# Gate and up projections of a two-layer diffusion block: eight-product pairs first, weight sums earlier, seven activations split ahead

## The chip, the cores and the metric

One core of one Trainium2 chip runs the whole program. The metric is the device time of one execution in microseconds (us).

## The reference, cut to what matters

The reference is a two-layer transformer block for 512 latent and 256 context tokens with a model width of 1024. Each layer normalises and modulates the tokens, mixes them with two attention branches, and adds a gated SwiGLU feed-forward with 2816 inner channels:

```python
def swiglu(h, w_gate, w_up, w_down):
    return (jax.nn.silu(h @ w_gate) * (h @ w_up)) @ w_down
...
h2 = modulate(rms_norm(x, norm2_g[l]), sh2, sc2)
x = x + gt2 * swiglu(h2, w_ffn_gate[l], w_ffn_up[l], w_ffn_down[l])
```

Layer 0 does this for 768 tokens, layer 1 (the last) for the 512 latent ones. The change lies in `h @ w_gate`, `h @ w_up` and in the passage to `@ w_down`.

## The kernel before, in words

Each layer runs `mixers` (projections and attention), `merge`, `project` (the output projection, one half of the tokens after the other), `gate_up` and `down`. Every matrix product is made of three matmuls on operands split into a high and a low part: ScalarE (ACT) copies the high part, VectorE (DVE) subtracts it from the value to get the low part. The order of the work on each engine is written out by hand, and each engine and each queue works through its own list in order.

The 22 tiles of 128 inner channels are called pairs here: gate tile f and up tile f. Two token halves (384 columns each in layer 0, 256 in layer 1) times gate and up make a 2x2 block, and `gate_up` computes it by a scheme of seven products in place of eight. A product is 12 matmuls (`prod`, line 1282; four tiles of the inner dimension, three matmuls each). The scheme needs sums and differences of weights, `prep_s` (DVE, lines 1330 and 1331) and `prep_s2` (GpSimd, POOL, lines 1336 and 1337, in place on the raw gate weights, so it has to wait until `prep_g` has read them), and sums and differences of the two token halves, the operands T1 to T4 (lines 1450 to 1455, 1516). Their splits are `prep_g`, `prep_13`, `prep_24` and `prep_a22` for weights, `high` and `low` (lines 1227 to 1232) for tokens. The evacuations are `ev_...`; S[f] holds a pair's tiles.

When `project` ends, the first token half is already normalised (`norm_half`: operands 11 and 21), the second is not. So lines 1459 to 1539 begin with the products of four pairs (`EARLY`) that need 11 and 21 alone, and prepare meanwhile everything else: `times` normalises the second half, `diff` forms the differences, then T2, T3, 22, T1, T4 follow. The loop over f (line 1558) comes after that; up to f = 3 it has an order of its own (`early`, `mixed`), from f = 4 one iteration issues on TensorE (PE) q6, r7, q5 of pair f, p1 of pair f+1, p3 of f, p2 of f+1, r4 of f. In it `prep_s(nf)` stands behind `prep_a22(f)`, `prep_s2(nf)` behind q5, and `prep_24(nf)`, which splits the result for the next q6, behind p1.

A finished pair is stored to DRAM (`store`, on the SyncE queue, SP). In the last pairs the first five (`AHEAD`) are read back and split (`act`); `down` reads pairs 5 and 6 back, then eight residual tiles `x`, then the first tiles of the next group, and runs three groups of pairs times eight output tiles (`down_group`). Raw weights lie in three slots "wf" that the weight queue `W`, the raw gate tiles and, in layer 0, the `ada` tiles share: `background` reads one `ada` tile (modulation weights of later stages, 56 of them in `ada_tiles`) and makes its dot products on DVE for the tile before. Layer 0's `down_group` runs all that are left ahead of the last group (line 1198).

Of the kernel before, what the change touches and what calls it, by code (L numbers as in the profile page):

```python
# [19 lines left out]
P = 128  # L20
# [14 lines left out]
EARLY = 4  # L35
AHEAD = 5
# [85 lines left out]
class Kernel:  # L122
# [60 lines left out]
    def weight_order(self, l):  # L183
        a, W = self.a, self.W
        idx = {m: i for i, m in enumerate([0, 1, 2, 3, 4, 6, 7, 8, 9, 10] + list(range(12, 28)))}
        win = lambda m: W.add(a["w_in"][l, idx[m]])
        for m in (4, 0, 1, 2):
            win(m)
        for m in range(2):
            W.add(a["w_v"][l, m])  # L190
        for m in (3, *range(12, 20), 10, 6, 7, 8, 9, *range(20, 28)):
            win(m)
        for m in range(8):
            W.add(a["w_proj"][l, m])
        for _ in range(2):
            for m in range(8):
                W.add(a["w_out"][l, m])
        if FAST[l]:
            for f in range(EARLY):
                W.add(a["w_gu"][l, 2 * f])  # L200
        for g, (f0, fn) in enumerate(GROUPS):
            for f in range(2 * f0, 2 * (f0 + fn)):
                if not FAST[l]:
                    W.add(a["w_gu"][l, f])
            for _ in range(2 if g == len(GROUPS) - 1 else 1):
                for m in range(8):
                    W.add(a[f"w_dn{g}"][l, m])
# [1038 lines left out]
    def norm_half(self, l, n, c0, c1):  # L1246
# [3 lines left out]
        self.H = {op: [None] * 4 for op in ("11", "21", "22", "T1", "T2", "T3", "T4")}  # L1250
# [22 lines left out]
    def gate_up(self, l, last, n, tq):  # L1273
# [81 lines left out]
        def q6(f):  # L1355
            early = f < EARLY
            if early:
                S[f]["a"] = self.wide("a")[:, :hw]
            prod(S[f]["a"], S[f]["S24"], 0, "T2", early)
# [31 lines left out]
        def ev_sum(f, cs):  # L1391
            if cs is lo_:
                S[f]["t"] = self.unit("t")
            t = S[f]["t"][:, cs]
            if f < EARLY:
                nc.vector.tensor_tensor(t, S[f]["a"], S[f]["s"][:, hi_], ALU.add)
            else:
                nc.scalar.activation(t, S[f]["a"], AF.Copy)
# [9 lines left out]
        def ev_c12(f):  # L1408
            s = S[f]["s"][:, hi_]
            if f < EARLY:  # L1410
                nc.vector.tensor_tensor(s, S[f]["a"], s, ALU.add)
                s = S[f]["s"][:, :n]
                nc.scalar.activation(s, s, AF.Silu)
            else:
                nc.scalar.activation(s, S[f]["a"], AF.Silu)
# [11 lines left out]
        ws = {}  # L1427

        def first(f, k):
            if k == 0:  # L1430
                ws[f] = self.W.get(1 if f < 2 else -1)
                S[f]["e"] = self.bank("e")[:, :hw]
            prod(S[f]["e"], ws[f], 512 * k, "21" if k else "11", k == 0)

        def first_evac(f, k):
            if k == 0:
                S[f]["s"] = self.unit("s")
            nc.scalar.activation(S[f]["s"][:, lo_ if k else hi_], S[f]["e"], AF.Copy)

        t, tt = [None] * KD, []  # L1440

        def times(i, eng=nc.scalar):
            t[i] = (self.tq.tile([P, hw], F32, name=self.nm("t"), tag="t", bufs=15) if i < KD - 1 else self.unit("t"))[:, :hw]
            nc.vector.tensor_tensor(t[i], xt[i][:, c0:c1], rb[:, :hw], ALU.mult)
            self.modulated(l, i, t[i], c0, c1, eng)
            nc.sync.dma_start(out=self.xs[i][:, :n], in_=xt[i][:, :n])
            xt[i] = None

        def diff(j):
# [7 lines left out]

        J = range(4)
        first(0, 0)
        load_g(0)  # L1460
        load_u(0)
        load_u(1)
        first_evac(0, 0)
        self.flush()
        r = self.stats(c0, c1)
        first(1, 0)
        first_evac(1, 0)
        rb = self.spread(r, c0, c1)
        prep_s(0)
        prep_s2(0)  # L1470
        first(0, 1)
        first(1, 1)
        for i in (0, 4, 1, 5):
            times(i)
        first_evac(0, 1)
        self.W.split(self.W.at + 1)
        times(2)
        times(6, nc.gpsimd)
        diff(0)
        times(3)  # L1480
        times(7, nc.gpsimd)
        load_g(1)
        first_evac(1, 1)
        self.low("T2", 0, t0[0], hw)
        diff(1)
        first(2, 0)
        first_evac(2, 0)
        diff(2)
        new_24(0)
        split_high(S[0]["G"], S[0]["S24"])  # L1490
        self.low("T2", 1, t0[1], hw)
        first(3, 0)
        diff(3)
        self.low("T2", 2, t0[2], hw)
        first_evac(3, 0)
        self.low("T2", 3, t0[3], hw)
        split_low(S[0]["G"], S[0]["S24"])
        load_g(2)
        first(2, 1)
        first(3, 1)  # L1500
        new_13(0)
        split_high(S[0]["S"], S[0]["S13"])
        for j in J:
            self.high("T3", j, t[j], hw)
            self.low("T3", j, t[j], hw)
        first_evac(2, 1)
        split_low(S[0]["S"], S[0]["S13"])
        q6(0)
        r7(0)
        first_evac(3, 1)  # L1510
        for j in J:
            self.high("22", j, t[j + 4], hw)
            self.low("22", j, t[j + 4], hw, nc.gpsimd)
        ev_sum(0, lo_)
        for j in J:
            nc.gpsimd.tensor_tensor(t0[j + 4], t0[j + 4], t0[j], ALU.add)
            self.high("T1", j, tt[j], hw)
            self.low("T1", j, tt[j], hw)
        nc.scalar.activation(S[0]["t"][:, hi_], S[0]["d"], AF.Copy)
        prep_a22(0)  # L1520
        prep_s(1)
        prep_s2(1)
        q5(0)
        s, t_ = S[0]["s"][:, hi_], S[0]["t"][:, hi_]
        nc.vector.tensor_tensor(t_, t_, S[0]["a"], ALU.subtract)
        nc.vector.tensor_tensor(t_, t_, s, ALU.subtract)
        p3(0)
# [3 lines left out]
        prep_24(1)  # L1531
        tq.close()
        ev_c12(0)
        r4(0)
        prep_13(1)
        q6(1)
        ev_diff(0, lo_)
        ev_act(0)
        ev_sum(1, lo_)
        prep_s(2)  # L1540
        prep_s2(2)
        prep_24(2)
        r7(1)
        load_g(3)

        with self.tc.tile_pool(name="pa", bufs=1, side="right", reuse_waits="tile") as pa:
            raw = {}

            def prefetch(i):
                raw[i] = pa.tile([P, TOK], F32, name=self.nm("ar"), tag="ar", bufs=AHEAD)  # L1550
# [7 lines left out]
            for f in range(1, NF):  # L1558
                early, mixed = f < EARLY - 1, f < EARLY
                end = f == NF - 1  # L1560
                nf = f + 1
                if not mixed:

                    q6(f)
                    if end:
                        act(0)
                    silu1(f)
                    ev_diff(f - 1, lo_)
                    prep_g(nf)
                    r7(f)  # L1570
                    ev_sum(f, lo_)
                    ev_act(f - 1)
                    prep_a22(f)
                    prep_s(nf)
                    if end:
                        act(1)
                    q5(f)
                    prep_s2(nf)
                else:
                    q5(f)  # L1580
                    if f > 1:
                        ev_diff(f - 1, lo_)
                        ev_act(f - 1)
                    prep_a22(f)
                self.background(0 if last else 1)
                if early:
                    q6(nf)
                elif nf < NF:
# [3 lines left out]
                if end:  # L1592
                    self.W.prepare()
# [3 lines left out]
                if end:  # L1597
                    act(2)
                p3(f)
                if early:  # L1600
                    ev_sum(nf, lo_)
                    if f + 2 == EARLY:
                        prep_g(f + 2)
                    prep_s(f + 2)
                    r7(nf)
                elif nf < NF:
                    ev_s1(nf)
                    if not mixed:
                        prep_24(nf)
                    p2(nf)  # L1610
                ev_c12(f)
                if early:
                    prep_s2(f + 2)
# [3 lines left out]
                self.background(0 if last else f % 2 or f >= 12)  # L1617
                r4(f)
                if early:
                    prep_24(f + 2)  # L1620
                elif nf < NF:
                    ev_c11(nf)
                load_g(f + 3)
                store(f - 1)
                if f >= NF - AHEAD - 2 and f < NF - 2:
                    prefetch(f - (NF - AHEAD - 2))
            act(4)
            ev_diff(NF - 1, lo_)
            ev_act(NF - 1)
            store(NF - 1)  # L1630
# [3 lines left out]
    def down(self, l, last, n, chunks, halves, streams):  # L1634
# [16 lines left out]
        for f in range(AHEAD, first):  # L1651
            load(f)
        self.xt = []
        for m in range(8):
            x = self.unit("x")
            nc.sync.dma_start(out=x[:, :n], in_=self.xs[m][:, :n])  # L1656
            self.xt.append(x)
        for f in range(first, first + 2):
            load(f)
        for f in range(AHEAD, first):  # L1660
            ready(f)
        self.rate = int(not last)
        for g, (f0, fn) in enumerate(GROUPS):
            act, self.act = self.act[:fn], []

            def step(m):
                f = f0 + fn + m
                if g + 1 < len(GROUPS) and m < GROUPS[g + 1][1]:
                    load(f + 2)
                    ready(f)  # L1670
            self.down_group(l, last, chunks, halves, streams, g == len(GROUPS) - 1, act, step)
        if last:
# [104 lines left out]
```

## Time and profile before

| what | value |
|---|---|
| runs | 1983.65, 1981.83, 1981.61 us, median 1981.83 |
| the profiled execution | 1985.74 us, its span 1984.0 us |
| busy | PE 1854.6 us (93%), DVE 1411.3 (71%), ACT 978.0 (49%), POOL 696.1 (35%) |
| granted TensorE clock, mean | 0.972 of full speed |
| `gate_up`, layer 0 and layer 1 | from 597.8 to 958.5 us and from 1559.7 to 1839.1 us of the span |
| HBM traffic | 228.02 MB read, 34.34 MB written |

Times inside the program are us from the start of the span. PE is the engine with the most work, so what counts is where it stands idle or runs at the lower of its two clock levels (1.2 and 2.4 GHz); the 93% is a mean over stages in which it never waits and stages in which it waits often.

### The profile page before, as it was taken

The page shows a single profiled execution, that of the slowest core. Times are in us where ns is not written, and L with a number is a line of the kernel's source. Part 1 is how long each engine was busy: PE and PEld are TensorE (multiplying, and loading weights), DVE is VectorE, ACT ScalarE, POOL GpSimd, SP SyncE. Part 2 cuts the span into 40 slices and gives each one's busy share as a digit, 9 for nine tenths or more (in the row PEclk, how much of TensorE's full clock was granted, in tenths as well). Part 3 has the DMA queues.
Part 4 walks back from the last instruction along what each step waited for, and adds up shares of the span by engine and source line. Part 5 has one row for each costly group of instructions (what it writes and reads, how often), then busy time and mean ns, then how long its engine had stood idle before and what let it go on. Part 6 is the DMA issues. An engine that isn't in the chain of part 4 may idle for free. (4 is left out here: it accounts for less than half of the span.)

```text
span 1984.0 us, 31045 instructions
## 1 busy us (share of the span) xinstructions
PE 1854.6 (93%) x11680; PEld 1754.3 (88%) x11680; DVE 1411.3 (71%) x2403; ACT 978.0 (49%) x1851; POOL 696.1 (35%) x662
## 2 busy tenths in 40 slices
PE   7999999999997899999899999999999869989898
PEld 3889899989997799999799998888889869888688
DVE  6668878995567789998666576758866766666445
ACT  5458736775345243334322345857864534444333
POOL 3446536552245123222000353536523522332003
PEclk7999999999998899999899999999999979999999
DMA  7222232225433344556665532122145533333544
GB/s 277 94 98 83 89 114 82 68 70 207 139 124 141 122 150 151 153 176 203 242 205 171 164 129 77 59 68 70 43 148 186 173 101 107 119 132 124 201 133 138
DMA packets 86612, 264.37 MB, mean 133 GB/s; under 512 B 9744, under 2 KB 11824, under 8 KB 86336
## 3 DMA queue, kind: packets, MB, share of 16 engines
q1 hardware_dynamic: 79280, 248.68, 38.1%
q10 hardware_dynamic: 6992, 13.64, 1.8%
q8 instruction: 92, 1.51, 0.3%
q0 software_dynamic: 192, 0.08, 0.1%
q14 instruction: 56, 0.46, 0.1%
HBM read 228.02 MB, written 34.34 MB: 132 GB/s over the span
## 5 line engine op out<-in xcount | busy, mean ns | idle before, releaser
L73 ACT ACTIVATE wh<-wf 128x1024 fp32r<-128x1024 f32 (+1 forms) x175 | 181.6, 1039 | 254.5 <-PE d L575 147.7
L74 DVE TENSOR_TENSOR wl<-wf,wh 128x1024 fp32r<-128x1024 f32 (+1 forms) x141 | 174.0, 1235 | 93.3 <-ACT wh L73 91.1
L573 PE MATMUL d<-hh,wl 128*128 128x384 f32 (+2 forms) x640 | 235.7, 368 | 0.6 <-DVE q L849 0.4
L574 PE MATMUL d<-hl,wh 128*128 128x384 f32 (+2 forms) x640 | 224.5, 351 | 1.0 <-DVE hl L543 0.9
L575 PE MATMUL d<-hh,wh 128*128 128x384 f32 (+2 forms) x640 | 223.9, 350 | 0.0
L573 PE MATMUL d<-ah,wl 128*128 128x384 f32 (+2 forms) x592 | 201.2, 340 | 14.7 <-ACT ah L179 10.3
L1336 POOL TENSOR_TENSOR rawG<-rawG,S 128x512 f32<-128x512 f32 x44 | 71.7, 1629 | 394.6 <-DVE S L1331 195.1
L574 PE MATMUL d<-al,wh 128*128 128x384 f32 (+2 forms) x592 | 200.5, 339 | 1.7 <-DVE al L180 1.7
L575 PE MATMUL d<-ah,wh 128*128 128x384 f32 (+2 forms) x592 | 199.7, 337 | 0.0
L484 POOL TENSOR_TENSOR ssq<-ssq,sq 128x384 f32<-128x384 f32 (+1 forms) x48 | 68.3, 1423 | 355.3 <-ACT sq L480 339.5
L812 POOL TENSOR_SCALAR p<-p,rec 128x768 f32<-128x768 f32 (+3 forms) x160 | 131.5, 835 | 94.5 <-DVE rec L809 65.5
L459 DVE SCALAR_TENSOR_TENSOR junk<-wa,crow 128x1024 bf16<-128x1024 f32 x128 | 159.1, 1243 | 3.3 <-DMA wa<-w_ada 3.3
L1124 DVE SCALAR_TENSOR_TENSOR x<-d,mod,x 128x384 f32<-128x384 f32 (+3 forms) x144 | 70.5, 509 | 123.2 <-PE d L575 123.2
L1289 PE MATMUL a<-H,wh 128*128 128x384 f32 (+1 forms) x640 | 143.6, 314 | 0.0
L868 DVE TENSOR_TENSOR pt<-pt,pt 128x512 fp32r<-128x512 f32 (+1 forms) x192 | 123.9, 661 | 25.2 <-ACT pt L864 24.0
L573 PEld LDWEIGHTS d<-ah,wl 128*128 128x128 f32 x592 | 113.4, 192 | 21.0 <-ACT ah L179 11.1
L575 PEld LDWEIGHTS d<-hh,wh 128*128 128x128 f32 x640 | 121.0, 189 | 7.4
L574 PEld LDWEIGHTS d<-hl,wh 128*128 128x128 f32 x640 | 121.8, 190 | 5.3 <-DVE hl L543 2.2
L573 PEld LDWEIGHTS d<-hh,wl 128*128 128x128 f32 x640 | 121.7, 190 | 5.2 <-issue 0.9
L864 ACT ACTIVATE pt<-pt 128x512 fp32r<-128x512 f32 (+1 forms) x192 | 107.2, 577 | 31.5 <-PE pt L827 27.4
L749 POOL TENSOR_TENSOR qs<-q,qs 64x128 fp32r<-64x128 f32 x160 | 81.1, 507 | 116.0 <-ACT qs L748 54.6
L574 PEld LDWEIGHTS d<-al,wh 128*128 128x128 f32 x592 | 113.6, 192 | 8.0 <-DVE al L180 3.5
(239 smaller groups left out, 5447.6 us busy)
## 6 DMA issues: line engine op xcount, KB each, us to landing
wa<-w_ada SPq DMA_DIRECT2D x96, 512.0 KB, 3.6
wf<-w_in SPq DMA_DIRECT2D x52, 512.0 KB, 3.5
rawG<-w_gu SPq DMA_DIRECT2D x44, 512.0 KB, 4.7
rawU<-w_gu SPq DMA_DIRECT2D x44, 512.0 KB, 3.8
wf<-w_out SPq DMA_DIRECT2D x32, 512.0 KB, 3.5
wf<-w_dn SPq DMA_DIRECT2D x32, 512.0 KB, 3.5
wf<-w_dn SPq DMA_DIRECT2D x32, 448.0 KB, 4.5
act_scratch<-s SPq DMA_DIRECT2D x22, 384.0 KB, 4.9
```

Of the source, the lines that this page charges most:

```text
L73: high = lambda: self.nc.scalar.activation(hi[:, :n], t[:, :n], AF.Copy)
L74: low = lambda: (engine or (self.nc.vector if self.aux is None else self.nc.gpsimd)).tensor_tensor(lo[:, :n], t[:, :n], hi[:, :n], ALU.sub ...
L459: nc.vector.scalar_tensor_tensor(junk, t, 1.0, self.crow[:, s, :], ALU.mult, ALU.mult, accum_out=acc)
L573: nc.tensor.matmul(ps, wl[:, ks], xh[:, c0:c1], start=first, stop=False)
L574: nc.tensor.matmul(ps, wh[:, ks], xl[:, c0:c1], start=False, stop=False)
L575: nc.tensor.matmul(ps, wh[:, ks], xh[:, c0:c1], start=False, stop=last)
L749: nc.gpsimd.tensor_tensor(st[l0:l0 + 64, c], q[h0:h0 + 64], st[h0:h0 + 64, c], ALU.subtract)
L812: nc.gpsimd.tensor_scalar(pt, pt, rec[:, i:i + 1], 1.0, ALU.mult, ALU.mult)
L864: nc.scalar.activation(r[1][0], r[0], AF.Copy)
L868: nc.vector.tensor_tensor(r[1][1], r[0], r[1][0], ALU.subtract)
L1289: nc.tensor.matmul(ps, a[:, ks], b, start=first and j == 0 and i == 0, stop=j == 3 and i == 2, skip_group_check=True)
L1336: nc.gpsimd.tensor_tensor(G[:, :512], G[:, :512], s[:, :512], ALU.subtract)
```

## The change

In both layers pairs 0 and 1 (`PLAIN`) are computed with the usual eight products (`plain`: one weight tile, one token half, eight inner tiles, 24 matmuls), pairs 2 to 21 with seven. The two token halves need only their own normalised values for that, as operands 11, 21, 12 and 22; T1 to T4 and the weight sums come after. The special order for the first pairs goes away. In the loop `prep_s(nf)` moves to just behind q6(f) and `prep_s2(nf)` behind `prep_g(nf)`. In the last pair seven activations are split in place of five, through five raw slots; `down` then reads only two `x` tiles at first, one more at each step, and stores the last pair after those first loads. The `ada` tiles start at pair 4, run on through all three groups of `down` in layer 0, and are no longer run out ahead of the last group.

```diff
-EARLY = 4
-AHEAD = 5
+PLAIN = 2
+AHEAD = 7
+SLOTS = 5
...
-            for f in range(EARLY):
-                W.add(a["w_gu"][l, 2 * f])
+            for f in range(2 * PLAIN):
+                W.add(a["w_gu"][l, f])
...
         if end and not last:
-            self.background(len(self.bg) + 1)
-            self.rate = 0
+            while len(self.bg) > 32:
+                self.background(1)
...
+        def plain(i, half, ws, ps=None):
+            ps = self.bank("d")[:, :hw]
+            for k in range(KD):
+                x = H[("11", "12", "21", "22")[half + k // 4 * 2]][k % 4]
...
+                nc.tensor.matmul(ps, wl[:, ks], x[:, lo_], start=k == 0, stop=False)
+                nc.tensor.matmul(ps, wh[:, ks], x[:, hi_], start=False, stop=False)
+                nc.tensor.matmul(ps, wh[:, ks], x[:, lo_], start=False, stop=k == KD - 1)
...
+        w = [self.W.get(2 - i) for i in range(3)]
+        g = plain(0, 0, w[0])
+        for _ in range(4):
+            next(g)
+        load_g(PLAIN)
+        load_u(PLAIN)
+        load_u(PLAIN + 1)
+        self.flush()
+        r = self.stats(c0, c1)
+        drain(g)
+        evs.popleft()()
+        rb = self.spread(r, c0, c1)
+        g = plain(1, 0, w[1])
+        for k in range(KD + 2):
+            if k < KD:
+                times(k, (nc.gpsimd, nc.scalar)[k % 2])
+            if 1 <= k <= KD:
+                self.high("12" if k <= 4 else "22", (k - 1) % 4, t[k - 1], hw)
+            if k >= 2:
+                self.low("12" if k < 6 else "22", (k - 2) % 4, t[k - 2], hw)
+            if k == 2:
+                drain(g)
+            if k == 5:
+                evs.popleft()()
+                drain(plain(2, 0, w[2]))
...
+        jobs = [plain(i, 1, w[i]) for i in range(2)]
+        for k in range(KD + 1):
+            for g in jobs:
+                next(g, None)
+        drain(plain(2, 1, w[2]))
...
+        for i in range(KD):
+            spill(i)
...
+        self.W.split(self.W.at)
+        store(0)
+        load_g(PLAIN + 1)
+        prep_s(PLAIN)
+        prep_g(PLAIN)
+        prep_s2(PLAIN)
         for j in J:
+            nc.gpsimd.tensor_tensor(t0[j + 4], t0[j + 4], t0[j], ALU.add)
             self.high("T3", j, t[j], hw)
             self.low("T3", j, t[j], hw)
...
+        drain(plain(3, 0, w3))
         for j in J:
             self.high("T1", j, tt[j], hw)
             self.low("T1", j, tt[j], hw)
+        evs.popleft()()
+        drain(plain(3, 1, w3))
...
+        p1(PLAIN)
+        prep_24(PLAIN)
+        prep_13(PLAIN)
+        evs.popleft()()
+        store(1)
+        ev_s1(PLAIN)
+        p2(PLAIN)
...
+            for f in range(PLAIN, NF):
...
+                bg = not last and PLAIN + 2 <= f and not end
+                q6(f)
+                if end:
+                    act(0)
+                    prefetch(SLOTS)
+                prep_s(nf)
+                silu1(f)
+                if f > PLAIN:
                     ev_diff(f - 1, lo_)
+                prep_g(nf)
+                prep_s2(nf)
+                r7(f)
+                ev_sum(f, lo_)
...
+            for i in range(4, AHEAD):
+                act(i)
...
+            self.stored = lambda: store(NF - 1)
...
+        load_x()
+        load_x()
         for f in range(first, first + 2):
             load(f)
-        for f in range(AHEAD, first):
-            ready(f)
+        self.stored()
...
             def step(m):
+                load_x()
...
+                if not last and m % 2:
+                    self.defer(2.2, lambda: self.background(1))
```

## Rows read from the trace of the kernel before

**Rows 1.** Busy time by stretch: from:to length, then PE, PEld, DVE, ACT, POOL, granted clock, DMA.
```profile
597.80:690.00 92.20, 71.93 (x353) 68.31 (x352) 70.58 (x100) 38.83 (x65) 33.45 (x27) 0.87 0.40 140
690.00:958.50 268.50, 265.75 (x1518) 262.56 (x1517) 239.74 (x340) 106.70 (x165) 69.70 (x34) 1.00 0.52 163
958.50:980.00 21.50, 13.17 (x63) 11.84 (x63) 6.85 (x10) 3.33 (x5) 0.00 (x0) 0.76 0.87 314
1559.70:1640.00 80.30, 58.33 (x393) 55.34 (x392) 55.84 (x90) 34.67 (x65) 28.07 (x27) 0.85 0.36 123
1640.00:1839.10 199.10, 180.92 (x1472) 177.27 (x1471) 125.72 (x177) 93.77 (x161) 58.81 (x34) 1.00 0.37 120
1839.10:1862.00 22.90, 16.75 (x58) 12.44 (x57) 10.82 (x15) 7.24 (x11) 0.00 (x0) 0.85 0.79 272
```

**Rows 2.** Timeline of PE in layer 0: start, length, line, operands.
```profile
597.82 0.33 PE L1289 MATMUL e<-H,wl 128*128 128x384 f32 x1
...
599.90 0.28 PE L501 MATMUL st<-ones,ssq 128*128 128x1 f32 x2
...
958.49 0.33 PE L573 MATMUL d<-ah,wl 128*128 128x384 f32 x1
```

**Rows 3.** Timeline of PE in layer 1.
```profile
1559.71 0.28 PE L1289 MATMUL e<-H,wl 128*128 128x256 f32 x1
...
1561.15 0.28 PE L501 MATMUL st<-ones,ssq 128*128 128x1 f32 x2
...
1839.12 0.40 PE L573 MATMUL d<-ah,wl 128*128 128x512 f32 x1
```

**Rows 4.** Waits of PE from 1640 to 1835: total, times, longest.
```profile
PE a L1289 <- DVE wl L180: 9.1, 9, 1.1
PE a L1289 <- DVE vl L180: 8.6, 8, 1.1
```

**Rows 5.** Timelines around one pair of layer 1, and issue to landing there.
```profile
1698.30 0.33 SPq L1304 DMA_DIRECT2D rawU<-w_gu  x1
...
1699.61 1.29 POOL L1336 TENSOR_TENSOR rawG<-rawG,S 128x512 f32<-128x512 f32 x1 [7.88 <-ACT t L1398]
...
1700.98 2.15 POOL L1337 TENSOR_TENSOR rawG<-rawG 128x512 f32<-128x512 f32 x1
...
1703.17 1.06 ACT L179 ACTIVATE vh<-rawG 128x1024 fp32r<-128x1024 f32 x1 [2.27 <-POOL rawG L1337]
...
1705.54 0.39 PE L1289 MATMUL a<-H,vl 128*128 128x256 f32 x1 [1.07 <-DVE vl L180]
...
1709.72 0.33 SPq L1304 DMA_DIRECT2D rawU<-w_gu  x1
...
rawU<-w_gu SPq DMA_DIRECT2D x16, 512.0 KB, 3.9
```

**Rows 6.** Timeline of DVE at the start of `gate_up`, both layers.
```profile
604.92 1.94 DVE L1444 TENSOR_TENSOR t<-x,rb 128x384 f32<-128x384 f32 x4
...
622.81 1.22 DVE L1310 TENSOR_TENSOR vl<-rawG,vh 128x1024 fp32r<-128x1024 f32 x1
...
623.94 1.95 DVE L1232 TENSOR_TENSOR H<-t,H 128x384 fp32r<-128x384 f32 x4
...
628.67 4.67 DVE L1232 TENSOR_TENSOR H<-t,H 128x384 fp32r<-128x384 f32 x4
...
1580.10 1.42 DVE L1232 TENSOR_TENSOR H<-t,H 128x256 fp32r<-128x256 f32 x4
...
1582.91 3.26 DVE L1232 TENSOR_TENSOR H<-t,H 128x256 fp32r<-128x256 f32 x4
```

**Rows 7.** Timelines of ACT and PE at the passages to the down projection and inside it.
```profile
968.65 0.84 ACT L179 ACTIVATE ah<-ar 128x768 fp32r<-128x768 f32 x1 [9.25 <-DMA ar<-act_scratch]
...
969.55 0.69 PE L573 MATMUL d<-ah,wl 128*128 128x384 f32 x1 [6.83 <-ACT ah L179]
...
1096.52 0.66 PE L573 MATMUL d<-ah,wl 128*128 128x384 f32 x1 [1.98 <-DVE wl L74]
```

More of the change, by code (lines that the diff above doesn't have):

```diff
@@ L1456, in diff @@
             self.high("T2", j, t0[j], hw)
[L1458 to L1495, printed above, removed]
-        self.low("T2", 3, t0[3], hw)
@@ L1517, in gate_up @@
+        w3 = self.W.get(-1)
+        drain(plain(3, 0, w3))
+        for j in J:
             self.high("T1", j, tt[j], hw)
             self.low("T1", j, tt[j], hw)
[L1519 to L1527, printed above, removed]
+        evs.popleft()()
@@ L1557, in gate_up @@
             self.act = []
[L1558 to L1559 removed]
+            for f in range(PLAIN, NF):
                 end = f == NF - 1
                 nf = f + 1
[L1562 to L1567, printed above, removed]
[L1568 to L1588 removed]
+                bg = not last and PLAIN + 2 <= f and not end
[6 more added lines that the diff above has]
+                if f > PLAIN:
+                    ev_diff(f - 1, lo_)
+                prep_g(nf)
+                prep_s2(nf)
+                r7(f)
+                ev_sum(f, lo_)
+                if f > PLAIN:
+                    ev_act(f - 1)
+                prep_a22(f)
+                if end:
+                    act(1)
+                    prefetch(SLOTS + 1)
+                q5(f)
+                self.background(int(bg))
+                if nf < NF:
                     p1(nf)
@@ L1616, in gate_up @@
                     self.W.prepare()
-                self.background(0 if last else f % 2 or f >= 12)
+                self.background(int(bg and f % 2))
                 r4(f)
-                if early:
-                    prep_24(f + 2)
-                elif nf < NF:
+                if nf < NF:
                     ev_c11(nf)
                 load_g(f + 3)
[L1624 to L1628, printed above, removed]
+                if f == NF - 2:
+                    for i in range(2):
+                        self.W.load(self.W.at + i)
+                if f > PLAIN:
+                    store(f - 1)
+                if NF - SLOTS - 2 <= f < NF - 2:
+                    prefetch(f - (NF - SLOTS - 2))
+            for i in range(4, AHEAD):
+                act(i)
+                if i == 5:
+                    ev_diff(NF - 1, lo_)
             ev_act(NF - 1)
-            store(NF - 1)
+            self.stored = lambda: store(NF - 1)
         self.H = None
@@ L1650, in down, with load_x @@
         first = GROUPS[0][1]
-        for f in range(AHEAD, first):
-            load(f)
         self.xt = []
[L1654 to L1657, printed above, removed]
+        def load_x():
+            m = len(self.xt)
+            if m < 8:
+                x = self.unit("x")
+                nc.sync.dma_start(out=x[:, :n], in_=self.xs[m][:, :n])
+                self.xt.append(x)
+        load_x()
+        load_x()
         for f in range(first, first + 2):
             load(f)
-        for f in range(AHEAD, first):
-            ready(f)
+        self.stored()
         self.rate = int(not last)
```

108 lines of the change are left out of this document (36 added, 72 removed).

## The prediction

> **What bounds the kernel now.** I read the summary first: PE is busy 93% of the span, so no other engine bounds the whole, and the question is where PE is not at full work. A table of busy time by stretch [rows 1] answers it. The long middle of layer 0's gate and up stage (690 to 958.5) has PE busy 265.75 of 268.50 us at full clock: only less work would help there. The start of that stage has PE busy 71.93 of 92.20 us at a granted clock of 0.87, the same start in layer 1 58.33 of 80.30 at 0.85, layer 1's middle 180.92 of 199.10 at full clock, and the two passages to the down projection 13.17 of 21.50 and 16.75 of 22.90 [rows 1].
>
> Next, what a stage would take without waits. Twelve matmuls of 384 columns, one product, take 599.90 - 597.82 = 2.08 us [rows 2], 0.1733 each; twelve of 256 columns 1561.15 - 1559.71 = 1.44 us [rows 3], 0.12 each. The stage has 22 x 7 products = 1848 matmuls.
> - Layer 0: 958.49 - 597.82 = 360.7 us [rows 2] against 1848 x 0.1733 = 320.3: an excess of 40.4 us.
> - Layer 1: 1839.12 - 1559.71 = 279.4 us [rows 3] against 1848 x 0.12 = 221.8: an excess of 57.6 us.
> - Passages: 63 matmuls in 21.5 us [rows 1] need 10.9, an excess of 10.6 in layer 0; in layer 1 58 matmuls of 512 columns need at most 58 x 0.24 = 13.9 of 22.9 us, an excess of 9.0.
>
> The list of waits and the timelines say what ends the idle time. In layer 1's middle PE waits 17 times for the low half of a weight split, 17.7 us in all [rows 4]. The timeline of one pair [rows 5] shows the chain: POOL's two weight sums start at 1699.61, take 1.29 and 2.15 us, ACT's split copy follows at 1703.17, DVE's subtraction after it, and PE resumes at 1705.54, 1.07 us late. A pair takes 1709.72 - 1698.30 = 11.42 us against 7 x 1.44 = 10.08. At the passage PE waits 6.83 us for ACT, and ACT for an activation read back from DRAM [rows 7].
>
> **The change, part by part.** *More matmuls.* Two pairs take eight products: 2 x 12 more matmuls a layer, 24 x 0.1733 = 4.2 us and 24 x 0.12 = 2.9 us, certain and on the path.
>
> *The start.* Before U1 (the second up tile) is needed PE now has six plain halves of 24 matmuls, none of which uses a difference: 144 x 0.1733 = 25.0 us and 2 us of statistics and spread, so it needs U1 split 27.0 us in. DVE begins about 6.5 us in (its first multiply stands at 604.92 [rows 6], behind 1.2 us of weight sums that move away). It has eight multiplies (3.9 at 1.94 for four), twelve `low` (5.9 at 1.95 for four), eight differences (about as the multiplies, 3.9), one product (0.5) and U1's low half (1.22) [rows 6]: 15.3 us. At the share DVE reached in this stretch, 70.58 of 92.20 [rows 1], that is 20.0, so 26.5 us in; the end is serial besides (the last T2 copy, a SiLU, U1's copy on ACT, then DVE), so I take a wait of 2.5, between 0 (DVE without pauses) and 6.
>
> Then PE has 72 matmuls (U1 twice, p1, p2: 12.5 us) before q6 of pair 2. DVE has two weight sums and two splits (3.7), a product (0.5) and eight `low`: 3.9 us alone, 9.3 us if they run as the four at 628.67 did, 4.67 us [rows 6]; together 8.1 to 13.5, a wait of 0 to 1.0; I take 0.5. q5 of pair 2 then needs an ACT copy that stands behind a SiLU and a split, which stand behind DVE's next split, product, four `low` and sum: 1.22 + 0.5 + 1.95 + 0.5 + 2 = 6.2 against two products, 4.2: a wait of 2.0. With 1.5 us at the lower clock level after a wait this makes 6.5 us of new waits in layer 0 (0 to 15).
>
> Layer 1 in the same way: PE needs U1 at 144 x 0.12 + 2 = 19.3 us. DVE's ops are 1.42 for four [rows 6], 11.5 us in all, 16.6 at its share of 55.84 in 80.30 [rows 1], from 4.7 us on, so 21.3 and the serial end: a wait of 3. PE's next 8.6 us stand against 7 to 10.6 (3.26 for four beside POOL [rows 6]): 1.2. Then 5.3 against 2.9: 2.4. With 2.5 at the lower clock 9.1 us (2 to 18). In both layers about 2 us (1.6) of statistics and 0.5 us of waits in the last pair stay.
>
> Layer 0: 40.4 - 4.2 - 6.5 - 2.0 - 0.6 = **27.1** us gained.
>
> *The weight sums in the loop.* `prep_s(nf)` moves past the difference, the products and the A22 split on DVE; `prep_s2` now starts once DVE has read the raw gate weights for A1. Counted from the start of q6 in layer 1, DVE ends the sums at about 0.3, the A1 low half at 1.9, and POOL works from there to about 5.4, in place of 1699.61 - 1705.54 + 11.42 = 5.5 to 9.0 [rows 5]. The split copy then waits for nothing but p1's evacuation (5.8), DVE ends the last low half at about 8.4, and PE needs it at 10.08. So the 1.34 us a pair go, 17 times. Nothing new is late: the raw up tile, requested behind the A22 split at about 4.5, lands 3.9 us later [rows 5], at 8.4, and DVE asks for it at 9.1. In layer 0, with 14.6 us a pair, there is nothing to gain in the loop and more cover.
>
> Layer 1: 57.6 - 2.9 - 9.1 - 1.6 - 0.5 = **43.5** us gained.
>
> *The passage.* Pairs 5 and 6 are read during the last pair, the eight `x` reads no longer go ahead of the next activations on SP, and the last store, whose data come late, goes behind them. What stays is the splitting of the last two activations on ACT and DVE, each about as long as PE's three matmuls: 1.5 and 1.0 us. If the two reads come no earlier the whole excess stays. Gain 10.6 - 1.5 + 9.0 - 1.0 = **17.1** us.
>
> *The modulation tiles.* Ahead of layer 0's last down group four were run out together, PE waited 1.98 us and resumed with matmuls at 0.66 in place of 0.33 [rows 7], at most another 2 us. Now they go with every step; some seven remain for the last group, beside shorter steps (24 matmuls, 4.2 us), against DVE's 1.4 us each. I take a gain of **2**, between -2 and 3.8. Their earlier load on DVE in the gate stage shrinks; PE was covered there anyway [rows 1].
>
> **Sum.** 27.1 + 43.5 + 17.1 + 2 = 89.7 us. The profiled execution took 1985.7 us, the median of the runs 1981.8, 3.9 less: 1896.0 and 1892.1. I predict 1892.
>
> **The rivals.**
> - *No new waits at the start.* DVE runs without pauses, as its busy sums alone would allow: 6.5 + 9.1 + 1.5 less, about 1875. Against it: in both starts of before DVE was at 77 and 70% only [rows 1].
> - *A dearer start.* The serial steps between ACT, DVE and POOL pause more often and half of the old excess beyond the loop stays, some 18 us in each layer in place of 6.5 and 9.1: 20 more, 1912. For it speaks that the old start lost as much with the same engines.
> - *DVE becomes the bound in layer 1's pairs.* DVE works 125.72 x 11.42 / 199.10 = 7.2 us a pair [rows 1, 5]. POOL's second sum took 2.15 us where the first took 1.29 [rows 5], while DVE made a split; the new place of the sums lies beside two DVE operations with two inputs from SBUF. If each POOL sum held DVE up for its 1.29, and the pauses that DVE keeps within a pair (about 1 us, while it waits for evacuations) stayed, a pair would take 7.2 + 2.6 + 1 = 10.8 instead of 10.08, and 18 pairs 13 us: 1905. By the Trainium skill (SBUF — State Buffer, section Who interferes with whom) such a DVE instruction and a GpSimd one that reads SBUF exclude each other, and whichever starts second is blocked until the first ends. The trace agrees in the 2.15 us; that rule would make this rival the outcome if POOL started first both times.
> - *The last activations still late.* The reads wait for a raw slot and the passages keep their excess: 17 more, 1909.
> - *Slower.* The raw up tile is now the first thing that DVE waits for in a pair, ahead of the difference, the A1 split and the POOL sums. Each us that it lands after 9.1 holds all of these. Layer 1 has 1.7 us of cover; to eat the whole gain its 18 pairs must lose 5 us each, so the tile would have to land about 11 us after its request. At 12 us the sum is near 2000. Against it: 3.9 us to landing [rows 5] and a DMA share of 0.37 [rows 1].
>
> **How the numbers follow.** Chances: my forecast (within 10 us of 1892) 0.57, no new waits 0.10, dearer start 0.17, DVE bound 0.08, activations late 0.05, slower 0.03. A measurement here can tell about 0.2% (4 us) from no change. Every case but the last is faster by more than that; a mixture of several bad cases could end level: faster 0.95, same 0.02, slower 0.03. The range goes from the case without new waits, 1874, to a dearer start with another of the bad cases in part, 1922; beyond it lie the slower case and the sums of two.
>
> **What would show it.** Right: in the changed profile PE is busy over 95% in the first 90 us of each gate stage, with waits of a few us for U1's low half and around pair 2; no waits for `wl` or `vl` in layer 1's middle, pairs of 10.1 us; the passages without a wait of 3 us or more; no wait at the start of layer 0's last down group. Wrong: new waits for DVE of over 20 us at the starts, pairs of layer 1 above 10.5 us, or reads of activations that PE still waits for.

## The result and the profile after

The changed kernel takes 1891.05 us (median) against 1982.74, a ratio of 0.9528, 95% interval 0.9507 to 0.9550: 94 us faster (89 to 98). One of its four runs was disturbed (3256 us); the ratio leaves it out, the median counts it. The profiled run took 1887.15 us, its span 1885.4, granted clock 0.990. Line numbers differ from the kernel before: products of the seven-product scheme stand at L1290 (L1289 before), plain ones at L1424 to L1426, those of the down projection at L574 to L576 (L573 to L575 before).

Busy time by stretch after the change, cut at the same kinds of work as [rows 1] (from:to length, PE, PEld, DVE, ACT, POOL, granted clock, DMA):

```profile
595.90:688.00 92.10, 89.14 (x517) 88.21 (x516) 67.25 (x89) 43.33 (x76) 32.05 (x27) 1.00 0.35 119
688.00:927.00 239.00, 238.42 (x1376) 238.10 (x1375) 217.29 (x307) 98.33 (x151) 53.74 (x31) 1.00 0.51 160
927.00:939.00 12.00, 11.38 (x64) 10.58 (x63) 8.83 (x13) 4.84 (x7) 0.00 (x0) 1.00 0.89 314
1516.90:1597.00 80.10, 75.79 (x615) 75.12 (x614) 68.11 (x102) 43.63 (x84) 29.85 (x27) 0.98 0.40 131
1597.00:1750.30 153.30, 152.83 (x1274) 152.62 (x1273) 122.38 (x152) 81.58 (x141) 46.23 (x28) 1.00 0.44 141
1750.30:1764.00 13.70, 13.70 (x63) 11.34 (x62) 8.82 (x13) 5.65 (x9) 0.00 (x0) 1.00 0.79 276
```

PE is busy 97% of the first stretch of layer 0 (78% before, at a clock of 0.87) and 95% of layer 1's (73%, at 0.85). Layer 1's middle lacks 0.5 us, where 18 lay before. In layer 0's passage 64 matmuls take 12 us where 63 took 21.5; in layer 1's PE never stops.

In these first stretches PE's waits added up to 20.2 us in layer 0 and 21.9 in layer 1 in the kernel before. The three largest of layer 0 (total, times, longest):

```profile
PE a L1289 <- DVE t L1396: 5.3, 2, 2.7
PE e L1289 <- ACT s L1438: 4.5, 2, 3.7
PE a L1289 <- DVE t L1525: 4.1, 1, 4.1
```

What is left after the change, PE's waits in the whole of the two stages, layer 0:

```profile
PE a L1290 <- ACT t L1392: 1.9, 2, 1.3
PE d L1424 <- DVE wl L75: 1.2, 1, 1.2
PE a L1290 <- DVE vl L181: 0.5, 1, 0.5
```

and layer 1:

```profile
PE a L1290 <- ACT t L1392: 2.1, 2, 1.6
PE d L1424 <- DVE wl L75: 1.9, 1, 1.9
PE a L1290 <- DVE vl L181: 0.6, 1, 0.6
```

The three waits of the start are the ones forecast: U1's low half, the split for pair 2's q6, and the evacuation ahead of its q5. (Of the two waits for `t` in each layer, the shorter one, 0.6 and 0.5 us, belongs to the last pair.)

### The profile page after: what moved, and what is told of

It is laid out like the page before. It is cut to its first block, busy times and chain, and to the rows that moved or that the text cites. A ratio compares the mean times of both kernels' runs of the same rounds, so it can differ in the third digit from the quotient of the medians.

```text
span 1885.4 us, 31055 instructions
## 1 busy us (share of the span) xinstructions
PE 1824.3 (97%) x11728; PEld 1737.0 (92%) x11728; DVE 1409.4 (75%) x2379; ACT 971.3 (52%) x1847; POOL 666.6 (35%) x652
## 4 chain that ended last, share of the span: by engine, by line
PE 67%; DVE 4%; ACT 2%; issue 1%; POOL 1%; DMA 1%; POOLq 0%; ACTq 0%; DVEq 0%
PE a L1290 15%; PE d L574 9%; PE d L575 9%; PE d L576 9%; PE d L1290 7%; PE b L1290 4%; PE av L839 2%; PE pr L576 2%; PE pr L575 2%; PE pr L574 2%; PE pt L828 2%; DVE H L1233 1%; PE S L764 1%; PE S L765 1%; DVE wl L75 1%
## 5 line engine op out<-in xcount | busy, mean ns | idle before, releaser
L75 DVE TENSOR_TENSOR wl<-wf,wh 128x1024 fp32r<-128x1024 f32 (+1 forms) x141 | 174.2, 1236 | 84.7 <-ACT wh L74 83.2
L574 PE MATMUL d<-hh,wl 128*128 128x384 f32 (+2 forms) x640 | 236.5, 370 | 0.6 <-DVE q L850 0.4
L575 PE MATMUL d<-hl,wh 128*128 128x384 f32 (+2 forms) x640 | 225.3, 352 | 0.9 <-DVE hl L544 0.9
L576 PE MATMUL d<-hh,wh 128*128 128x384 f32 (+2 forms) x640 | 225.0, 352 | 0.0
L460 DVE SCALAR_TENSOR_TENSOR junk<-wa,crow 128x1024 bf16<-128x1024 f32 x128 | 179.4, 1402 | 31.3 <-DMA wa<-w_ada 31.1
L574 PE MATMUL d<-ah,wl 128*128 128x384 f32 (+2 forms) x592 | 197.9, 334 | 1.3 <-DVE wl L75 1.3
L575 PE MATMUL d<-al,wh 128*128 128x384 f32 (+2 forms) x592 | 197.7, 334 | 0.6 <-DVE al L181 0.5
L576 PE MATMUL d<-ah,wh 128*128 128x384 f32 (+2 forms) x592 | 197.4, 333 | 0.0
L1290 PE MATMUL a<-H,wh 128*128 128x384 f32 (+1 forms) x640 | 140.0, 308 | 0.0
L1125 DVE SCALAR_TENSOR_TENSOR x<-d,mod,x 128x384 f32<-128x384 f32 (+3 forms) x144 | 69.6, 509 | 79.2 <-PE d L576 79.2
L576 PEld LDWEIGHTS d<-hh,wh 128*128 128x128 f32 x640 | 121.6, 190 | 7.6
L575 PEld LDWEIGHTS d<-hl,wh 128*128 128x128 f32 x640 | 122.4, 191 | 5.6 <-DVE hl L544 2.3
L574 PEld LDWEIGHTS d<-hh,wl 128*128 128x128 f32 x640 | 122.3, 191 | 5.4 <-issue 0.9
L574 PEld LDWEIGHTS d<-ah,wl 128*128 128x128 f32 x592 | 111.7, 189 | 6.3 <-DVE wl L75 2.0
L575 PEld LDWEIGHTS d<-al,wh 128*128 128x128 f32 x592 | 111.7, 189 | 5.8 <-DVE al L181 1.4
```

The source lines that it names most:

```text
L75: low = lambda: (engine or (self.nc.vector if self.aux is None else self.nc.gpsimd)).tensor_tensor(lo[:, :n], t[:, :n], hi[:, :n], ALU.sub ...
L460: nc.vector.scalar_tensor_tensor(junk, t, 1.0, self.crow[:, s, :], ALU.mult, ALU.mult, accum_out=acc)
L574: nc.tensor.matmul(ps, wl[:, ks], xh[:, c0:c1], start=first, stop=False)
L575: nc.tensor.matmul(ps, wh[:, ks], xl[:, c0:c1], start=False, stop=False)
L576: nc.tensor.matmul(ps, wh[:, ks], xh[:, c0:c1], start=False, stop=last)
L1290: nc.tensor.matmul(ps, a[:, ks], b, start=first and j == 0 and i == 0, stop=j == 3 and i == 2, skip_group_check=True)
```

## The experiments

Each trace was cut at the same three matmuls: the first of either stage's gate work and the first of either down projection. "Between" runs from layer 0's down projection to layer 1's stage, "tail" from layer 1's down projection to the end, both in us. The stretch ahead of layer 0's stage, which no kernel touches, took 595.4 to 600.6 us: a whole span is not surer than that, a stage is (layer 0's came out at 331.1 to 331.2 in nine traces that leave it as changed). "Between" is less sure than a stage: one stretch of it, behind the down projection, takes 24.9 us in the changed kernel (granted clock 1.00) and 26.4 in e5, e10, e11 and e12 (0.94 in e10).

| kernel | ratio, 95% interval | layer 0 stage | between | layer 1 stage | tail |
|---|---|---|---|---|---|
| before | | 360.7 | 601.2 | 279.4 | 144.9 |
| changed | 0.9528, 0.9507 to 0.9550 | 331.2 | 589.9 | 233.4 | 135.1 |
| e1 sums back | 0.9646, 0.9625 to 0.9668 | 331.2 | 589.4 | 259.0 | 134.6 |
| e2 sums alone | 0.9879, 0.9861 to 0.9898 | 358.8 | 602.8 | 257.5 | 143.0 |
| e3 start alone | 0.9800, 0.9782 to 0.9818 | 331.2 | 612.7 | 259.5 | 142.3 |
| e4 passage back | 0.9606, 0.9586 to 0.9627 | 331.1 | 599.4 | 233.4 | 143.9 |
| e5 x first | 0.9609, 0.9596 to 0.9622 | 331.2 | 600.0 | 233.4 | 143.8 |
| e6 flush back | 0.9597, 0.9584 to 0.9610 | 331.2 | 605.6 | 233.4 | 135.3 |
| e7 sums on DVE | 0.9509, 0.9496 to 0.9522 | 330.0 | 589.4 | 232.1 | 134.6 |
| e8 tuned start | 0.9523, 0.9506 to 0.9539 | 330.5 | 590.0 | 234.1 | 135.1 |
| e9 store first | 0.9553, 0.9540 to 0.9566 | 331.2 | 592.8 | 233.4 | 139.8 |
| e10 eight x | 0.9554, 0.9541 to 0.9567 | 331.2 | 596.2 | 233.4 | 135.7 |
| e11 five ahead | 0.9548, 0.9535 to 0.9561 | 331.2 | 596.0 | 233.3 | 135.5 |
| e12 no POOL sums | 0.9531, 0.9518 to 0.9544 | 331.7 | 591.2 | 235.3 | 135.2 |

**e1 and e2: the weight sums, put back in the new kernel and moved alone in the old one.**

```diff
-                prep_s(nf)
                 silu1(f)
...
-                prep_s2(nf)
                 r7(f)
...
                 prep_a22(f)
+                prep_s(nf)
...
                 q5(f)
+                prep_s2(nf)
```

> The changed kernel with the weight sums of the loop put back: prep_s(nf) behind the A22 split, prep_s2(nf) behind q5. My theory: in layer 1 PE waits again for the low halves wl and vl once a pair and a pair goes from 10.08 back to about 11.4 us, 18 pairs, so 1891 + 24 = about 1915 us (0.966 of before); layer 0 stays. Rival, that the start of the stage and not the place of the sums freed the pairs (the raw tiles are now requested earlier, the old wait was a late tile): pairs stay at 10.1 us and the time at 1891 to 1894 us.

> The kernel of before with nothing changed but the places of prep_s(nf) and prep_s2(nf) in the loop. My theory: the 17 waits of 1.07 us mean in layer 1 go, pairs 11.42 to 10.08 us, 17 x 1.34 = 23 us off: about 1959 us (0.9885). Rival, that the chain from ACT's copy to DVE's subtraction only finds another thing to wait for in the old kernel: less than 10 us off, 1972 us or more.

e1: layer 1's stage 25.6 us longer, 1914 us. The waits of [rows 4] are back (PE from 1590 to 1770 us):

```profile
PE a L1290 <- DVE vl L181: 8.7, 8, 1.1
PE a L1290 <- DVE wl L181: 8.6, 8, 1.1
```

e2: layer 1's stage 21.9 us shorter, 1961 us, and from 1640 to 1810 us PE does not pause:

```profile
1640.00:1810.00 170.00, 170.00 (x1419) 170.00 (x1419) 136.64 (x168) 89.15 (x151) 55.23 (x34) 1.00 0.44 139
```

The place of the sums alone makes the loop's gain, in the old kernel as in the new; both rivals fall. The old loop forms 17 sums (pairs 5 to 21), the new one 19 (pairs 3 to 21): 17 x 1.34 = 22.8 and 19 x 1.34 = 25.5 us. In layer 0 e2 gained 1.9 us, e1 lost nothing.

**e3: the new start alone** (the edits of e1, e4 and e6 together).

> The new start of the stage alone: the changed kernel with the weight sums, the passage to the down projection and the modulation tiles ahead of layer 0's last group all as before. My theory, the parts add up: 27.1 us in layer 0 and 43.5 - 22.8 = 20.7 in layer 1, so 1982 - 48 = about 1935 us (0.976). Rival, that the new start needs the early sums (pair 2's weight sums stand in it, pair 3's come in the first turn of the loop): PE waits ten us and more there, 1945 us or more. Rival on the other side, that the start is worth more than I put it because the waits measured in it are 3 us a layer: 1925 us.

1945 us, ten more than by my theory, but not where the rival put them: the two stages are 29.5 and 19.9 us shorter, as the parts should add up. The ten lie between the stages, which grew by 11.5 us over the kernel before. e6 tells why.

**e6: the remaining modulation tiles run out ahead of layer 0's last down group, as before.**

```diff
-            while len(self.bg) > 32:
-                self.background(1)
+            self.background(len(self.bg) + 1)
```

> The changed kernel with all modulation tiles that are left run out ahead of layer 0's last down group, as before. My term: 2 us more (between 2 less and 3.8 more), so 1893. Rival, that the steps between the output tiles already leave so few tiles that nothing is to be run out: no difference, 1891. Rival, that the dot products beside the last group's steps cost more than one flush: 1888.

13 us more than the changed kernel, outside all three. PE, then two of the eight dot products on DVE:

```profile
1069.58 0.69 PE L574 MATMUL d<-ah,wl 128*128 128x384 f32 x1 [14.64 <-DVE wl L75]
```

```profile
1055.54 1.23 DVE L460 SCALAR_TENSOR_TENSOR junk<-wa,crow 128x1024 bf16<-128x1024 f32 x1 [1.34 <-DMA wa<-w_ada]
...
1058.24 1.22 DVE L460 SCALAR_TENSOR_TENSOR junk<-wa,crow 128x1024 bf16<-128x1024 f32 x1 [1.28 <-DMA wa<-w_ada]
```

The new kernel runs fewer of the tiles in the gate stage, where they start at pair 4 and the late pairs no longer all take two, so eight are left at this point, four before. Each holds DVE for 2.7 us here, 1.3 of them waiting for the tile's DMA, and the next weight's split stands behind all of them. So the flush that made PE wait 2.0 us in the old kernel [rows 7] would make it wait 14.6 in the new one: taking it out gains little against the kernel before, but without it the later start of the tiles would cost 13 us. e3's trace has the same wait, 14.9 us, and with it its ten.

**e4, e5, e9, e10, e11: the passage.** e4 restores it (five activations ahead, old queue). The others take its parts: e5 puts the last store and all eight `x` tiles first, e9 the store alone, e10 the eight tiles alone, and e11 keeps the new queue but splits only five ahead.

```diff
-        load_x()
-        load_x()
+        for m in range(8):
+            load_x()
         for f in range(first, first + 2):
             load(f)
```

(This is e10; in e9 and e5 `self.stored()` goes ahead of the first `load_x()`, in e5 with the loop of e10; e4 and e11 have `AHEAD = 5` and read pairs 5 and 6 in `down`.)

> The changed kernel with the old passage: five activations split ahead, the last store first, then reads of pairs 5 and 6, all eight x tiles, the next two. My theory: PE waits again some 6 us in layer 0 and 3 in layer 1 for a split activation and more at the lower clock level, 17 us in all: about 1908 us (0.9625). Rival, that the stage's faster last pair or the freed queue already brings the reads in time: under 6 us, 1897 us or less.

> The changed kernel with seven activations split ahead, but with the old order of the SyncE queue at the passage: the last store first, then all eight x tiles, then the next two activations. Theory, that splitting ahead is what counts: the next activations are not needed before the next group of the down projection, some 58 us later in layer 0, and the first x tile not before PE has done its first output tile, so 0 to 3 us more, 1891 to 1894. Rival, that the queue's order was the cost: 8 us or more, 1899 and up.

> The changed kernel with only the last store moved: it stands on the SyncE queue ahead of the two x tiles and the next two activations, not behind them. With the store and all eight x tiles first, the seventh activation's low half came at 945.65 us in place of 935.45 and PE waited 6.8 us in layer 0 behind DVE, which stood still for it. PE would therefore bear the low half some 3 us later than in the changed kernel. The store's data are ready at 932.0, so the four reads go out 6 us later than now. Theory, that it takes store and eight tiles together: 0 to 4 us more, 1891 to 1895. Rival, that the store's place alone is the cost: 10 us and more, 1901.

> The changed kernel with all eight x tiles ahead of the next two activations, the last store behind both, as now. Eight tiles are 3.1 MB, 9 us at the 350 GB/s of that stretch, six of them more than now ahead of the activation that DVE takes first: it comes about 6 us later. Theory, that it takes store and eight tiles together: 1 to 5 us more, 1892 to 1896. Rival, that the eight tiles alone are the cost: 12 us and more, 1903.

> The changed kernel with five activations split ahead, as before, but with the new queue: pairs 5 and 6, two x tiles, the next two activations, then the last store, and one x tile a step. PE has five pairs of products, 5.2 us in layer 0 and 3.4 in layer 1, until it needs pair 5, which is requested when the stage ends, lands 5.8 us later and takes 2 us to split. Theory, that splitting ahead saves those waits: 2 to 4 us in layer 0, 4 to 5 in layer 1, so 6 to 9 more, 1897 to 1900. Rival, that the queue's order is all that counted: within 3 us of 1891.

e4: 9.5 us between the stages and 8.8 in the tail, 18.3 in all, 1908 us; as predicted: PE waits 5.6 us for `ah` in layer 0 (6.83 in [rows 7]) and 3.6 in layer 1. e5 was a miss: with all seven activations split ahead the whole cost came back, 10.1 + 8.7 us. DVE and PE of e5 show it:

```profile
945.65 0.96 DVE L181 TENSOR_TENSOR al<-ar,ah 128x768 fp32r<-128x768 f32 x1 [13.63 <-ACT ah L180]
```

```profile
949.53 0.69 PE L574 MATMUL d<-ah,wl 128*128 128x384 f32 x1 [6.78 <-DVE x L1125]
```

The same operation of the changed kernel:

```profile
935.45 0.96 DVE L181 TENSOR_TENSOR al<-ar,ah 128x768 fp32r<-128x768 f32 x1 [3.14 <-ACT ah L180]
```

PE does not need this eighth activation (the seventh, counted from 0, in the expectation of e9) for a whole group yet. But DVE splits it ahead of the first output tile's residual (L1125), and PE waits for that residual, which by the profile is what sets its next output bank free. In layer 1 the same late split stands ahead of the next weight tile's low half on DVE, and PE waits 7.3 us for that (`wl`, L75). My expectation asked who reads the late tile, not who stands behind it.

Taken singly, the store's place (e9) costs 2.9 + 4.7 us by the traces, 1896 us; the eight tiles (e10) 6.3 + 0.5, 1896 us; five in place of seven (e11) 6.1 + 0.4, 1895 us, with PE waiting 2.0 us for `ah`. Some 1.5 us of e5's, e10's and e11's first number lie in the stretch behind the down projection and not at the passage. By the medians all three lie 4 to 5 us above the changed kernel; the intervals of the ratios still touch, and it is the stages in the table that tell them apart. e11 came out between my two values, e9 and e10 just above my theory's. The parts are no sum: e9 and e10 make 14 us by the traces, both at once 19. Layer 0 shows why. The eighth activation's low half begins 8.4 us after the start of the down projection in the changed kernel, 13.2 in e9, 14.6 in e10 and 18.9 in e5, and PE's first wait for the residual is 0, 1.1, 2.4 and 6.8 us: up to 12.1 us costs nothing, from there on every us late is a us of wait. Each of the two moves uses up the same slack of 3.7 us.

**e7: `prep_s2` on DVE in place of POOL.**

```diff
-                nc.gpsimd.tensor_tensor(G[:, :512], G[:, :512], s[:, :512], ALU.subtract)
-                nc.gpsimd.tensor_tensor(G[:, 512:], G[:, 512:], G[:, :512], ALU.add)
+                nc.vector.tensor_tensor(G[:, :512], G[:, :512], s[:, :512], ALU.subtract)
+                nc.vector.tensor_tensor(G[:, 512:], G[:, 512:], G[:, :512], ALU.add)
```

> The changed kernel with the two sums of prep_s2 on DVE in place of POOL. In layer 1's pairs the A22 subtraction on DVE takes 1.58 us beside POOL's sum and 0.69 without it in the kernel of before, so POOL's sums cost DVE 0.9 us a pair; on DVE they are two more operations of 0.69, 1.4 us. Theory, that DVE has room in layer 1 (113.2 us busy of 140): pairs stay at 10.08 us and the time within 2 us of 1891. Rival, that DVE's remaining pauses are fixed by the evacuations and it is at its bound: 0.5 us a pair in 18 pairs, 9 us more, 1900. In layer 0 no difference by either.

1886 us, both stages 1.2 to 1.3 us shorter, the pairs still at full pace (PE busy 140.00 of 140.00 us from 1600 on). The bound rival falls: DVE's busy time in that stretch rose from 113.2 to 119.0 us and PE did not feel it. The time is 5 us below my value, which gave neither stage a gain; whether e7 beats the changed kernel is not settled, as the intervals of the ratios overlap. The gains that the traces show lie in the starts and not in the pairs: in layer 0 PE waits 0.5 us in place of 1.3 for pair 2's evacuation and no longer 0.5 for its split, in layer 1 the same wait for U1 (1.86 us) is not followed by matmuls at the lower clock level (granted clock 1.00 in the ten us around it, 0.83 in the changed kernel).

**e8 and e12: the waits of the start.** e8 splits U1 ahead of the last T2 subtractions and evacuates pair 2's first sum earlier. e12 goes further: U1 still earlier, pair 2's second split ahead of T3 and T1, and all sums of POOL in the start and the loop on DVE.

```diff
         for j in J:
+            if j == 3:
+                self.W.split(self.W.at)
             nc.vector.tensor_tensor(t[j], t[j], t[j + 4], ALU.subtract)
...
-        self.W.split(self.W.at)
         store(0)
...
         prep_s2(PLAIN)
+        prep_24(PLAIN)
...
                 q6(f)
+                if f == PLAIN:
+                    ev_sum(f, lo_)
```

(The lines as in e12; T4's sums now stand ahead of its copies.)

> The changed kernel with two moves in the start: U1's split ahead of the last two T2 subtractions instead of behind all of them, and the evacuation of pair 2's first sum on ACT ahead of its SiLU and of the next gate split. PE waited for the first 1.15 us in layer 0 and 1.88 in layer 1, for the second 1.33 and 1.61, and in layer 1 ran about 15 matmuls near half speed after the first. Theory, that each was the wait that ended last: 6 to 8 us off, about 1884 us. Rival, that T2's last operand or pair 2's split is late next: 3 us or less, 1888 and up.

> The changed kernel with POOL's sums moved to DVE, those of the weights and those of T1 and T4 in the start (POOL's and DVE's operations held each other up there: eight T3 and T1 subtractions took 7.14 us beside POOL's sums and 2.76 in another run with DVE first, where POOL's sum took 3.75 in place of 1.39), U1's split ahead of the last T2 difference, pair 2's second split ahead of the T3 and T1 subtractions, and pair 2's first evacuation ahead of its SiLU. Theory, that the waits of the start go (3.0 us in layer 0, 4.1 and about 1.5 at the lower clock in layer 1): about 1882 us (0.949). Rival, that the moved waits only come back at the next operand, as in the run with two of these moves: 1886 us and up.

Both missed. e8: 1888 us, layer 0's stage 0.7 us shorter, layer 1's 0.7 longer; PE still waits 0.6 and 1.6 us for U1, and new waits for pair 2's splits, 1.4 us for `wl` in layer 0 and 2.2 for `vl` in layer 1 (0.6 in the changed kernel), stand behind it. e12: 1891 us, the stages 0.5 and 1.9 us longer. In e12 U1's wait is gone, but PE's waits in layer 1's stage now read:

```profile
PE a L1290 <- ACT t L1392: 2.6, 2, 2.1
PE a L1290 <- ACT s L1383: 2.2, 1, 2.2
PE a L1290 <- DVE wl L181: 0.3, 1, 0.3
```

The evacuations on ACT are late instead. ACT of e12:

```profile
1543.40 1.06 ACT L180 ACTIVATE vh<-rawG 128x1024 fp32r<-128x1024 f32 x1 [3.61 <-DVE rawG L1338]
...
1554.36 0.42 ACT L1230 ACTIVATE H<-t 128x256 fp32r<-128x256 f32 x1 [0.83 <-DVE t L1525]
```

With the earlier split of pair 2, ACT's copy `vh` waits 3.6 us for DVE's sum, and eight token copies and then the evacuation `s` stand behind it on ACT; T4's copies wait for DVE's new sums, with `t` behind them. The rivals hold: here a wait that was taken out came back at the next operand.

## Why the prediction was right, and where it was not

Forecast 1892 us, measured 1891. That they lie 1 us apart is partly luck: the terms add up to 89.7 us, the ratio says 94. Term by term, us gained:

| step | predicted | measured by traces |
|---|---|---|
| layer 0's stage | 27.1 | 29.5 |
| layer 1's stage, loop | 22.8 | 25.6 (e1), 21.9 (e2) |
| layer 1's stage, start | 20.7 | 20.4 (e1 against before), 19.9 (e3), or 24.1 (changed against e2) |
| passages | 17.1 | 18.3 (e4) |
| modulation tiles | 2 | 1.8 (11.3 between the stages less e4's 9.5) |
| sum | 89.7 | 98.6 for the two profiled runs, 94 by the ratio |

The rest of the 98.6 is 2.0 us ahead of the stage and 1.0 in the tail, about what the traces differ by anyway; the profiled run of before lay 3.9 us above the median of the runs first shown and that of the changed kernel 3.9 below its own. Layer 1's stage gained 46.0 us (43.5 forecast), which is 25.6 + 20.4 or 21.9 + 24.1, by the kernel in which the sums are moved.

- *The start.* The mechanism was right: most of the old waits went, and the three new ones are those forecast. e3 shows what the new start is worth as a whole; the plain products and the new order of the preparations were not tried apart. The new waits were put too long. Layer 0: 2.5, 0.5, 2.0 and 1.5 at the lower clock predicted; 1.2, 0.5, 1.3 and none measured. Layer 1: 3, 1.2, 2.4 and 2.5 against 1.9, 0.6, 1.6 and about 1.4. PE's first product with U1, in the two layers:

```profile
624.18 0.45 PE L1424 MATMUL d<-H,wl 128*128 128x384 f32 x1 [1.15 <-DVE wl L75]
...
1537.97 0.39 PE L1424 MATMUL d<-H,wl 128*128 128x256 f32 x1 [1.88 <-DVE wl L75]
```

  U1 was ready 624.18 - 595.86 = 28.3 us into the stage, forecast 27.0 + 2.5 = 29.5, and 1537.97 - 1516.92 = 21.1, forecast 22.3. That this came so close is luck in part, because two errors went against each other. From its first multiply to the end of U1's low half DVE was busy 19.1 of 21.9 us in layer 0 and 14.2 of 16.2 in layer 1, 87% and 88% of the time, where I had put 15.3 and 11.5 us of work at 77% and 70%: the operations took longer (two of the differences 1.37 us beside POOL's sums, in place of 0.55), and the pauses were shorter. The lower clock did not come in layer 0.
- *The loop.* Right: pairs of 10.08 us and no waits for `wl` or `vl`. The 17 turns are those of the old loop, and e2 gains 21.9 us there for 22.8 forecast. Put this way, the start gained 24.1 us, 3.4 more than forecast, about what its waits and its stretch at the lower clock fell short of the forecast (5.5 us in place of 9.1). e1 puts the two turns that the new loop has more into the loop instead.
- *The passages.* Right in size. I gave the earlier splitting and the queue's new order as one cause; the runs show that both are needed, and that with the old order what stands in the way is DVE's next work behind a late split: the first residual in layer 0, a weight tile's low half in layer 1. The changed kernel also requests the first weight tiles of the down projection earlier (in layer 0 16.7 us ahead of it, 13.4 before); no run takes that back alone.
- *The modulation tiles.* Right in size against the kernel before, wrong as a term of its own: I priced the four old tiles and never asked what the flush would cost with the eight that the later start leaves (14.6 us of wait, e6). The forecast that no wait stays at the last group's start was off by little: 1.1 us is left.
- *The rivals.* No new waits, dearer start and late activations did not come. DVE as the bound did not either, though its premise held in part. The subtraction in the kernel before, ahead of POOL's sums, then one pair of the new loop on DVE and POOL:

```profile
1697.59 0.69 DVE L180 TENSOR_TENSOR zl<-rawU,zh 128x512 fp32r<-128x512 f32 x1
```

```profile
1664.31 1.58 DVE L181 TENSOR_TENSOR zl<-rawU,zh 128x512 fp32r<-128x512 f32 x1
```

```profile
1663.67 1.68 POOL L1337 TENSOR_TENSOR rawG<-rawG,S 128x512 f32<-128x512 f32 x1 [6.70 <-DVE wl L181]
1665.42 1.62 POOL L1338 TENSOR_TENSOR rawG<-rawG 128x512 f32<-128x512 f32 x1
```

The subtraction that takes 0.69 us alone took 1.58 beside the sum: 0.9 us a pair lost, as a mean over 14 pairs too. What failed in this rival is the price of the hold-up (7.2 + 2.6 + 1): POOL's sums cost DVE 0.9 us a pair and not 2.6, and POOL was held up too (1.68 and 1.62 us in place of 1.29). With 0.9 the same sum gives 9.1 us, below PE's 10.08, and DVE indeed had 140 - 113.2 = 26.8 us free from 1600 to 1740, 1.9 a pair. The slower rival never came near: the raw up tile landed 4.0 us after its request (3.9 before), and DVE's sum of it never waited.

## What to carry to other kernels

Find out which operation sits in front of the wait and whether its inputs exist earlier: moving the weight sums by a few lines was worth 23 to 24 us, in the old kernel as in the new. Where a late transfer is not needed soon, look at what is queued behind its first reader: at the passage a tile needed 58 us later stopped PE for 6.8. And price a part that a change removes at the amounts of the new kernel, not of the old: a flush that made PE wait 2 us would have cost 13.

## What the runs showed of the hardware

POOL and DVE hold each other up, and by the profile's start times which of them waits is not settled by which began first. Eight subtractions on DVE in layer 1's start, in the changed kernel beside POOL's sums, the second of the eight, and POOL's first sum:

```profile
1540.17 7.14 DVE L1233 TENSOR_TENSOR H<-t,H 128x256 fp32r<-128x256 f32 x8
```

```profile
1540.51 1.50 DVE L1233 TENSOR_TENSOR H<-t,H 128x256 fp32r<-128x256 f32 x1
```

```profile
1540.33 1.39 POOL L1337 TENSOR_TENSOR rawG<-rawG,S 128x512 f32<-128x512 f32 x1 [4.41 <-DVE wl L181]
```

The same eight and the same sum in e8:

```profile
1540.34 2.76 DVE L1233 TENSOR_TENSOR H<-t,H 128x256 fp32r<-128x256 f32 x8
```

```profile
1540.50 3.75 POOL L1337 TENSOR_TENSOR rawG<-rawG,S 128x512 f32<-128x512 f32 x1 [5.19 <-DVE wl L181]
```

In both, DVE's first subtraction began 0.16 us ahead of POOL's sum. In the changed kernel POOL's sum then kept its 1.39 us and DVE's second subtraction took 1.50, and the eight lasted until just after POOL's sums beside them; in e8 the eight went through and POOL's sum ended only after all of them. The exclusion agrees with the Trainium skill (SBUF — State Buffer, section Who interferes with whom), which has the two engines share a port pair under an exclusive lock. The prediction drew on it and on the rule there that whichever starts second waits; that rule alone does not tell these two runs apart, and what does the runs don't show. What I had not expected is how far it goes, a factor of 2.6 on DVE and of 2.7 on POOL.

The clock went to its lower level after a wait of 1.88 us in layer 1 but not after those of 1.15 and 1.33 us in layer 0, nor after the later one of 1.6 in layer 1. The length of the wait alone does not decide it: e7 has the same wait at the same place, 1.86 us, and stays at full clock, and in e10 PE stays there after a wait of 2.4 us for the residual in layer 0. PE of the changed kernel after U1's wait:

```profile
1539.86 0.41 PE L1424 MATMUL d<-H,wl 128*128 128x256 f32 x1
...
1540.50 0.41 PE L1424 MATMUL d<-H,wl 128*128 128x256 f32 x1
```

Three matmuls take 0.64 us, 0.213 each in place of 0.12, for some 15 matmuls (granted clock 0.50 from 1539.2 to 1542.4): 1.4 us. What sets when it falls was not tried.
